# Packing the gains into the first transfer, holding the third feature tile's transfer, the first norm in the fifth chunk, and smaller store pieces in a two-layer trunk

## The chip, the cores and the metric

The kernel runs on one core of a Trainium2 chip. The metric is the device time of one execution in microseconds. The engines are called by these names: TensorE (PE, with its weight loads PEld), VectorE (DVE), ScalarE (ACT), GpSimd (POOL) and SyncE (SP). SP does no arithmetic here; it issues the loads and most of the stores, one behind the other, each as soon as what it waits for is there.

## The reference

There are 256 tokens of width 2048, and 16 learned tokens are put ahead of them, so L = 272. Layer 0 is differential attention with 8 heads, a partial rotary embedding and a SiLU gate; layer 1 is causal pooling over windows of 2, 4, 8 and 16 with a SiLU gate. Everything is 32-bit floating point.

```python
for i in range(DEPTH):                       # DEPTH = 2
    hn = rms_norm(h, pre_norm_g[i])
    if i % N_MIXERS == 0:
        y = diff_attention_mixer(hn, attn_w_in[j], attn_w_out[j], ...)
    else:
        y = pool_mixer(hn, pool_w_in[j], pool_w_group[j], pool_scale[j], pool_w_out[j])
    h = h + rms_norm(y, post_norm_g[i])
return h[:, N_META:]
```

`rms_norm(x, g)` is x / sqrt(mean(x²) + eps) · g. In the attention, `lam = exp(sum(lq1*lk1)) - exp(sum(lq2*lk2)) + lam_init` weighs the second softmax against the first.

## The kernel before

**Layout.** Features lie on the 128 partitions: the residual stream is 16 feature tiles (KT = 16) of 128 x 272. A weight chunk is 128 output features of one projection, 128 partitions x 2048 columns, 1 MB; the list `chunks` (lines 57 to 71) holds all of them in the order of their use: per head two chunks of q, two of k and two of v, then 16 of the gate, 16 of the output projection, then those of layer 1.

**Precision.** A 32-bit product is made of three matmuls on a faster type. Each operand is split into a head, rounded by ScalarE (`act.copy`, line 97), and a remainder, which VectorE gets by subtraction (line 98). `mm3` (lines 119 to 123) multiplies head by head, head by remainder and remainder by head.

**Chunks.** `load(i)` (line 75) issues the transfer of chunk i into one of two raw buffers, `split(i)` (line 84) makes head and remainder, three buffers each. A raw buffer comes free when VectorE has made the remainder; only then can the load of the chunk after the next one start. `rest[i]` is the instruction that makes the remainder.

**The front.** The first four chunks (q0, q1, k0, k1: `FIRST`) can't be multiplied before the feature tiles are there, so they come mixed with them: the tensor `first` holds for each feature tile 272 columns of activations and 4 x 128 columns of weights. Lines 203 to 206 load it in eleven transfers: activations and first weight block of tile 0, the rest of tile 0, tiles 1, 2 and 3 singly, then six pairs of tiles. The constants, 70 columns of gains and lambda vectors (`small`), come by a transfer on ScalarE's queue into `sp` (line 140). Six small matmuls on a tile of ones (`busy(6)`, line 193; each is two instructions) run while the first transfer is under way; the ones are written by GpSimd (line 147).

For each feature tile k (lines 226 to 245) ScalarE casts the weights (230) and the activations times their gain (234), VectorE makes both remainders (231, 235), and TensorE issues twelve matmuls (239 to 241) into four accumulators. The squares of the activations for the first norm are made on ScalarE (`square0`, line 224) and added up by VectorE (`fold`, line 107; the last sum is line 255).

**The first norm.** The projections are linear in the token's norm factor, so the norm is applied behind them: to the rotary tables and the gates. Chunks 4 and 5 (`NF`, `NF + 1`: the two v chunks of head 0) run with `run_part(i, a, n)`, which issues the 3 n matmuls of feature tiles a to a + n - 1. `Norm` (lines 157 to 186) takes the mean by matmuls against a column of ones (171), scales it on VectorE (174), raises it to -0.5 on GpSimd (181), and spreads the result over the partitions by matmuls (185). Line 262 copies it out of PSUM as `r0`, and lines 264 and 265 multiply the rotary tables by it; nothing of head 0 can be evacuated before that. The order around it:

```python
run_part(NF, 0, KT)
run_part(NF + 1, 0, 5)
norm0 = Norm(sq0, "pre0", rcol0)
with tc.issue_after(norm0.vi.ins):
    split(NF + 2)
run_part(NF + 1, 5, 7)
dve.tensor_copy(r0, norm0.spread())
```

**Order.** The builder lists the instructions of each engine in an order of its own, by the text's order and by what is ready. `with tc.issue_after(ins)` puts the instructions of the block that run on the same engine as `ins` behind it there. On the chip each engine then works its list off in order.

**The main loop.** From slot 6 on (lines 504 to 529) each slot is one chunk: its 48 matmuls (`proj`), then the evacuation of its result and a step of an earlier head. Slots 0 to 5 have their results already in `acc0`; for them only the evacuation runs.

**The end.** Layer 1's output projection gives two blocks of 128 tokens. For the second block (b = 1, lines 776 to 796) columns 0 to 511 go through TensorE and ScalarE and are stored by ScalarE; VectorE makes the other 1536 columns in three pieces of 640, 512 and 384 (lines 793 to 795), and SP stores each.

Of the kernel before, what the change touches and what calls it, by code (L numbers as in the profile page):

```python
# [40 lines left out]


@with_exitstack
def trunk(ctx: ExitStack, tc: tile.TileContext, first, hT, xt, small, gpost1, rope, w_in, w_out, p_in, p_grp, p_out, out):
    nc = tc.nc
    dve, act, pool, pe = nc.vector, nc.scalar, nc.gpsimd, nc.tensor

# [36 lines left out]
    def split(i, parts=1, dst=None):  # L84

        if i >= NCH or i in halves:
            return
        load(i, parts)
        if dst is None:
            hi = wpool.tile([P, CW], F32R, tag="hi", name=f"hi{i}")  # L90
            lw = wpool.tile([P, CW], F32R, tag="lo", name=f"lo{i}")
        else:
            hi, lw = dst
        w = CW // parts
        for q in range(parts):
            s = slice(q * w, (q + 1) * w)
            act.copy(hi[:, s], raw[i][:, s])  # L97
            rest[i] = dve.tensor_tensor(out=lw[:, s], in0=raw[i][:, s], in1=hi.bitcast(F32)[:, s], op=ALU.subtract)  # L98
        halves[i] = (hi, lw)
# [32 lines left out]
    def busy(n):  # L132

        ps = bank("busy")
        for _ in range(n):
            pe.matmul(ps[:, 0:P], ones, ones, start=True, stop=True)


    sp = const.tile([P, C_END], F32, name="sp")
    act.dma_start(sp, small)  # L140
    rp = const.tile([P, 2, L], F32, name="rp")
    ident = const.tile([P, P], F32, name="ident")
    pool.memset(ident, 0.0)
    pool.affine_select(out=ident, in_=ident, pattern=[[-1, P]], compare_op=ALU.not_equal, fill=1.0,
                       base=0, channel_multiplier=1)
    ones = const.tile([P, P], F32, name="ones")
    pool.memset(ones, 1.0)
    warm = const.tile([P, 1], F32, name="warm")
    act.square(warm, ones[:, 0:1])
    ones_r = const.tile([P, P], F32R, name="ones_r")  # L150
    pool.tensor_copy(ones_r, ones)
    mhalf = const.tile([P, 3], F32, name="mhalf")
# [4 lines left out]
    class Norm:  # L157
# [10 lines left out]
        def mean(self, sq):  # L168
            c = 505 if self.v is None else 508
            for j in range(3):  # L170
                self.last = pe.matmul(self.pb[:, c + j:c + j + 1], sq[:, WIN[j]:WIN[j] + P], ones[:, 0:1], start=True, stop=True)
            v = const.tile([P, 3], F32, tag="nv", name=f"v_{self.name}_{c}", bufs=2)
            if self.v is None:
                self.vi = dve.tensor_scalar(out=v, in0=self.pb[:, c:c + 3], scalar1=1.0 / D, scalar2=EPS, op0=ALU.mult, op1=ALU.add)
            else:
                dve.scalar_tensor_tensor(out=v, in0=self.pb[:, c:c + 3], scalar=1.0 / D, in1=self.v, op0=ALU.mult, op1=ALU.add)
            self.v = v
# [12 lines left out]
    xs = base.tile([P, 2, KT, L], F32R, tag="xs", name="xs")  # L190
    xh, xl = xs[:, 0], xs[:, 1]

    busy(6)
    x0 = ExitStack()
    xp = x0.enter_context(tc.tile_pool(name="xp", bufs=1))
    sq0 = const.tile([P, L], F32, tag="sq", name="sq0")


    NF = len(FIRST)
    pk = xp.tile([P, KT, L + NF * P], F32, name="pk")  # L200
    fhi = base.tile([P, KT, NF, P], F32R, tag="os", name="fhi")
    flo = (base.tile([P, KT // 2, NF, P], F32R, tag="big", name="flo0"), xp.tile([P, KT // 2, NF, P], F32R, name="flo1"))
    nc.sync.dma_start(pk[:, 0, 0:L + P], first[:, 0, 0:L + P])
    nc.sync.dma_start(pk[:, 0, L + P:], first[:, 0, L + P:])
    for a, b in ((1, 2), (2, 3), (3, 4), (4, 6), (6, 8), (8, 10), (10, 12), (12, 14), (14, 16)):
        nc.sync.dma_start(pk[:, a:b, :], first[:, a:b, :])
    load(NF)
    nc.sync.dma_start(rp, rope)
    load(NF + 1)
# [16 lines left out]
    for k in range(KT):  # L226
        hi, lw = fhi[:, k], flo[k // 8][:, k % 8]
        for i, n in ((0, 1), (1, NF - 1)) if k == 0 else ((0, NF),):
            w = pk[:, k, L + i * P:L + (i + n) * P].rearrange("p (i c) -> p i c", c=P)
            act.copy(hi[:, i:i + n], w)  # L230
            dve.tensor_tensor(out=lw[:, i:i + n], in0=w, in1=hi.bitcast(F32)[:, i:i + n], op=ALU.subtract)
            if i == 0:
                g = sp[:, C_PRE0 + k:C_PRE0 + k + 1]
                act.activation(xh[:, k, :], pk[:, k, 0:L], AF.Copy, scale=g)
                dve.scalar_tensor_tensor(out=xl[:, k, :], in0=pk[:, k, 0:L], scalar=g, in1=xh.bitcast(F32)[:, k, :],
                                         op0=ALU.mult, op1=ALU.subtract)
        for i in range(NF):
            o = acc0[i][:, 0:L]
            pe.matmul(o, hi[:, i], xh[:, k, :], start=k == 0, stop=False)  # L239
            pe.matmul(o, lw[:, i], xh[:, k, :], start=False, stop=False)  # L240
            pe.matmul(o, hi[:, i], xl[:, k, :], start=False, stop=k == KT - 1)
        if k >= 8:
            square0(k - 8)
        if k >= KT - 2:
            split_part(NF, slice((k - KT + 2) * (CW // 2), (k - KT + 3) * (CW // 2)))
# [2 lines left out]
    fold(s8[:, 0:8], s8[:, 0])  # L248
    for k in range(8, KT):
        square0(k)  # L250
    split(NF + 1)
    load(NF + 3)
    with tc.issue_after(rest[NF + 1].ins):
        fold(s8[:, 8:KT], s8[:, 8])
        dve.tensor_tensor(out=sq0, in0=s8[:, 0], in1=s8[:, 8], op=ALU.add)
    run_part(NF, 0, KT)
    run_part(NF + 1, 0, 5)
    norm0 = Norm(sq0, "pre0", rcol0)
    with tc.issue_after(norm0.vi.ins):
        split(NF + 2)  # L260
    run_part(NF + 1, 5, 7)
    dve.tensor_copy(r0, norm0.spread())

    dve.tensor_tensor(out=rp[:, 0, :], in0=rp[:, 0, :], in1=r0, op=ALU.mult)
    dve.tensor_tensor(out=rp[0:ROPE, 1, :], in0=rp[0:ROPE, 1, :], in1=r0[0:ROPE, :], op=ALU.mult)
    run_part(NF + 1, 12, 4)
    x0.close()
    l0 = ExitStack()
    att = l0.enter_context(tc.tile_pool(name="att", bufs=1))
# [2 lines left out]
    on = base.tile([P, KT, L], F32, tag="big", name="on")  # L272
    ssb = att.tile([P, NH, L], F32, name="ssb")


    lp = const.tile([P, 2], F32, name="lp")
    dve.tensor_tensor(out=lp, in0=sp[:, C_LAM:C_LAM + 2], in1=sp[:, C_LAM + 2:C_LAM + 4], op=ALU.mult)
    psl = bank("psl")
    pe.matmul(psl[:, 0:2], ones, lp, start=True, stop=True)
    le = const.tile([P, 2], F32, name="le")  # L280
    act.activation(le, psl[:, 0:2], AF.Exp)
    dve.scalar_tensor_tensor(out=lamc, in0=le[:, 0:1], scalar=LAM_INIT, in1=le[:, 1:2], op0=ALU.add, op1=ALU.subtract)

    sub = const.tile([P, 2], F32, name="sub")
    dve.tensor_scalar(out=sub, in0=sp[:, C_SUB:C_SUB + 2], scalar1=1.0 - LAM_INIT, scalar2=None, op0=ALU.mult)
# [218 lines left out]
    for slot in range(NH * 6 + KT):  # L504
        if slot < NH * 6:
            h, i = divmod(slot, 6)
            hd = heads[h]
            if i == 0:
                hd.h = h
                hd.qk = att.tile([P, 4, L], F32, name=f"qk{h}", tag="qk")  # L510
                hd.qs = att.tile([P, 2, 4, L], F32R, name=f"qs{h}", tag="qs")
                hd.qkh, hd.qkl = hd.qs[:, 0], hd.qs[:, 1]
                hd.qm = att.tile([P, 2, 2, 32], F32R, name=f"qm{h}", tag="qm")
                hd.sw = att.tile([ROPE, 4, L], F32, name=f"sw{h}", tag="sw")
                hd.vT = att.tile([P, 2, L], F32, name=f"vT{h}", tag="vT")
        if slot < 6:
            ps = acc0[slot]
        else:
            ps = bank(f"p{slot}")
            proj(ps, 0, L, xh, xl)  # L520

        if slot == NF + 2:
            with tc.issue_after(heads[0].done.ins):
                split(cur[0] + 1)
        elif slot != NF + 3:
            split(cur[0] + 1)
        load(cur[0] + 2)
        with tc.issue_after(rest[cur[0]].ins):
            after_proj(slot, ps)
# [246 lines left out]
    def out_store(b, y_last):  # L776
        i = 3 + b
        r = rf[:, b:b + 1]
        act.activation(r, part_s[:, b, i:i + 1], AF.Sqrt, scale=1.0 / D, bias=rm[:, b:b + 1])
        y_last()  # L780
        dve.reciprocal(r, r)
        if b:

            c = slice(0, 512)
            po = [bank(f"po{q}")[:, 0:256] for q in range(2)]
            for q in range(2):
                pe.matmul(po[q], ident, ht[:, b, 256 * q:256 * q + 256], start=True, stop=False)
            act.activation(diag, ident, AF.Copy, scale=r)
            for q in range(2):
                pe.matmul(po[q], diag, y[:, b, 256 * q:256 * q + 256], start=False, stop=True)  # L790
                act.copy(ht[:, b, 256 * q:256 * q + 256], po[q])
            act.dma_start(out[b * P:(b + 1) * P, c], ht[:, b, c])
        for c in (slice(512, 1152), slice(1152, 1664), slice(1664, D)) if b else (slice(0, 512), slice(512, 1280), slice(1280, D)):
            dve.scalar_tensor_tensor(out=ht[:, b, c], in0=y[:, b, c], scalar=r, in1=ht[:, b, c],
                                     op0=ALU.mult, op1=ALU.add)
            nc.sync.dma_start(out[b * P:(b + 1) * P, c], ht[:, b, c])
# [41 lines left out]
def _cols(v):  # L838
    return np.ascontiguousarray(np.asarray(v).reshape(-1, P).T)
# [49 lines left out]
```

## Time and profile before

| | us |
|---|---|
| median of 3 runs | 838.74 |
| lowest and highest run | 838.42, 839.45 |
| the profiled execution | 839.03 |
| its span, first to last instruction | 837.2 |
| TensorE busy in the span | 828.8 |
| VectorE, ScalarE, GpSimd busy | 584.9, 433.9, 6.2 |
| data moved | 149.35 MB, mean 178 GB/s |

The mean granted TensorE clock of the profiled execution is 0.999 of full speed. A row of the timeline reads: start in us from the span's start, duration in us, engine, line, operation, output and inputs with their shapes, count; in brackets the idle time of the engine ahead of it and what ended it. A row of the stretches of time reads: from and to, length, busy time (and instructions) of PE, PEld, DVE, ACT and POOL, granted clock, mean busy share of the 16 DMA engines, GB/s. A row of the waits reads: who waited for whom, us in total, times, longest.

### The profile page before, as it was taken

What the parts mean: (1) busy time and instruction counts of PE and PEld (TensorE: products, weight loads), DVE (VectorE), ACT (ScalarE), POOL (GpSimd) and SP (SyncE); (2) the same over time, 40 slices, a digit from 0 to 9 for tenths busy, and PEclk for the clock granted to TensorE, in tenths of its full rate; (3) what the DMA queues carried; (4) which work ended last, traced back from release to release, by engine and by line L of the source; (5) the groups of instructions that cost most, each with busy time, mean ns of one, the idle gap of its engine ahead of it and who ended that gap; (6) DMA issues with size and microseconds to landing.
All of it is one profiled execution on the core that took longest, in us unless ns stands there. A gap on an engine that the chain in (4) does not pass through costs nothing.

```text
span 837.2 us, 14470 instructions
## 1 busy us (share of the span) xinstructions
PE 828.8 (99%) x6072; PEld 798.2 (95%) x6072; DVE 584.9 (70%) x953; ACT 433.9 (52%) x674; POOL 6.2 (1%) x14
## 2 busy tenths in 40 slices
PE   8999999999999999999999999999999999999997
PEld 8999999999999999999999999999999888888886
DVE  6789777676858687897854644797998766775423
ACT  7646655554545465855445543554544445564422
POOL 0100000000000000000000000000000000000000
PEclk9999999999999999999999999999999999999999
DMA  9445444444444444355459754146556555545512
GB/s 350 175 151 200 153 151 155 154 158 164 159 165 156 152 151 151 117 186 189 164 178 379 272 184 151 51 158 245 176 194 263 180 195 201 182 169 201 202 51 100
DMA packets 22385, 149.35 MB, mean 178 GB/s; under 512 B 2608, under 2 KB 2992, under 8 KB 5552
## 3 DMA queue, kind: packets, MB, share of 16 engines
q1 hardware_dynamic: 22032, 148.14, 49.2%
q8 instruction: 47, 0.77, 0.4%
q10 hardware_dynamic: 288, 0.30, 0.1%
q14 instruction: 18, 0.15, 0.1%
HBM read 146.33 MB, written 2.10 MB: 177 GB/s over the span
## 4 chain that ended last, share of the span: by engine, by line
PE 98%; DMA 1%; POOL 0%; DVE 0%; ACT 0%; issue 0%; SPq 0%; DVEq 0%; ACTq 0%; POOLq 0%
PE p L121 14%; PE p L122 14%; PE p L123 14%; PE pv L129 7%; PE py L121 4%; PE py L123 4%; PE py L122 4%; PE pu L122 4%; PE pu L121 4%; PE pu L123 4%; PE pv L130 4%; PE pz L759 3%; PE pz L758 3%; PE pz L760 3%; PE pm L129 2%; PE pq L239 1%
## 5 line engine op out<-in xcount | busy, mean ns | idle before, releaser
L98 DVE TENSOR_TENSOR lo<-raw,hi 128x2048 fp32r<-128x2048 f32 (+1 forms) x123 | 279.1, 2270 | 137.4 <-ACT hi L97 137.2
L97 ACT CAST hi<-raw 128x2048 fp32r<-128x2048 f32 (+1 forms) x123 | 233.0, 1896 | 193.0 <-PE p L122 95.3
L121 PE MATMUL p<-xs,hi 128*128 128x272 f32 x928 | 270.2, 291 | 0.0
L123 PE MATMUL p<-xs,lo 128*128 128x272 f32 x928 | 268.3, 289 | 0.0
L122 PE MATMUL p<-xs,hi 128*128 128x272 f32 x928 | 267.5, 288 | 0.0
L122 PEld LDWEIGHTS p<-xs,hi 128*128 128x128 f32 x928 | 174.8, 188 | 0.0
L121 PEld LDWEIGHTS p<-xs,hi 128*128 128x128 f32 x928 | 174.8, 188 | 0.0
L123 PEld LDWEIGHTS p<-xs,lo 128*128 128x128 f32 x928 | 174.6, 188 | 0.0
L129 PE MATMUL pv<-hs,hi 128*128 128x512 f32 x256 | 89.5, 393 | 0.0
L121 PE MATMUL py<-os,hi 128*128 128x272 f32 x256 | 74.3, 290 | 0.0
L123 PE MATMUL py<-os,lo 128*128 128x272 f32 x256 | 74.1, 289 | 0.0
L122 PE MATMUL py<-os,hi 128*128 128x272 f32 x256 | 73.7, 288 | 0.0
L130 PE MATMUL pv<-hs,lo 128*128 128x256 f32 x256 | 71.8, 280 | 0.0
L123 PE MATMUL pu<-hs,lo 128*128 128x260 f32 (+3 forms) x224 | 63.7, 285 | 0.0
L122 PE MATMUL pu<-hs,hi 128*128 128x260 f32 (+3 forms) x224 | 63.6, 284 | 0.0
L121 PE MATMUL pu<-hs,hi 128*128 128x260 f32 (+3 forms) x224 | 63.6, 285 | 0.0
L129 PEld LDWEIGHTS pv<-hs,hi 128*128 128x128 f32 x256 | 48.0, 188 | 10.9
L122 PEld LDWEIGHTS py<-os,hi 128*128 128x128 f32 x256 | 48.3, 189 | 0.0
L121 PEld LDWEIGHTS py<-os,hi 128*128 128x128 f32 x256 | 48.2, 188 | 0.0
L123 PEld LDWEIGHTS py<-os,lo 128*128 128x128 f32 x256 | 48.2, 188 | 0.0
L130 PEld LDWEIGHTS pv<-hs,lo 128*128 128x128 f32 x256 | 48.1, 188 | 0.0
L760 PE MATMUL pz<-hi,zs 128*128 128x512 f32 (+1 forms) x120 | 45.0, 375 | 0.0
(248 smaller groups left out, 1319.0 us busy)
## 6 DMA issues: line engine op xcount, KB each, us to landing
raw<-in_w_in SPq DMA_DIRECT2D x60, 1024.0 KB, 4.8
raw<-in_p_in SPq DMA_DIRECT2D x29, 1024.0 KB, 4.8
raw<-in_w_out SPq DMA_DIRECT2D x16, 1024.0 KB, 4.9
raw<-in_p_out SPq DMA_DIRECT2D x14, 1024.0 KB, 4.8
pk<-in_first SPq DMA_DIRECT2D x6, 784.0 KB, 11.4
raw<-in_p_grp SPq DMA_DIRECT2D x4, 1024.0 KB, 4.8
rawu<-in_p_in SPq DMA_DIRECT2D x3, 1024.0 KB, 6.5
h<-in_hT SPq DMA_DIRECT2D x4, 544.0 KB, 7.2
```

Of the source, the lines that this page charges most:

```text
L97: act.copy(hi[:, s], raw[i][:, s])
L98: rest[i] = dve.tensor_tensor(out=lw[:, s], in0=raw[i][:, s], in1=hi.bitcast(F32)[:, s], op=ALU.subtract)
L121: pe.matmul(o, wh, xh, start=first, stop=False)
L122: pe.matmul(o, wh, xl, start=False, stop=False)
L123: pe.matmul(o, wl, xh, start=False, stop=last)
L129: pe.matmul(ps[:, 0:2 * n], wh, x, start=first, stop=False, skip_group_check=not first)
L130: pe.matmul(ps[:, 0:n], wl, x[:, 0], start=False, stop=last)
L239: pe.matmul(o, hi[:, i], xh[:, k, :], start=k == 0, stop=False)
L758: pe.matmul(ps, zh[:, k, s], wh[:, c], start=k == 0, stop=False)
L759: pe.matmul(ps, zh[:, k, s], wl[:, c], start=False, stop=False)
L760: pe.matmul(ps, zl[:, k, s], wh[:, c], start=False, stop=k == KT - 1)
```

## The change

- The 70 columns of constants are packed in front of tile 0 in the tensor `first`; the transfer on ScalarE's queue is gone. The gains of the front are read from the packed tile, and GpSimd copies all 70 columns to `sp` for the later users.
- Ahead of the transfer of the third feature tile GpSimd copies one element of the first piece to where that transfer will write. So the transfer, and what follows on SP, waits until the first piece has landed.
- The ones are written by VectorE instead of GpSimd, the warm-up has seven matmuls instead of six, and ScalarE's first activation stands behind the transfers in the text.
- The last sums of the squares come ahead of chunk 5's remainder on VectorE; the mean of the first norm is taken after eight feature tiles of chunk 4, and its spread after five more. Chunk 6's remainder follows the copy of `r0`. The matmul, exponential and sum that give lambda move into that stretch.
- Chunk 7's load and head are issued in slot 0 and its remainder in slot 4.
- The second block's store pieces are 256, 512, 512 and 256 columns.

```diff
     sp = const.tile([P, C_END], F32, name="sp")
-    act.dma_start(sp, small)
     rp = const.tile([P, 2, L], F32, name="rp")
+    ones = const.tile([P, P], F32, name="ones")
+    dve.memset(ones, 1.0)
...
-    ones = const.tile([P, P], F32, name="ones")
-    pool.memset(ones, 1.0)
     warm = const.tile([P, 1], F32, name="warm")
-    act.square(warm, ones[:, 0:1])
...
-    busy(6)
+    busy(7)
...
-    pk = xp.tile([P, KT, L + NF * P], F32, name="pk")
+    pks = xp.tile([P, C_END + KT * (L + NF * P)], F32, name="pk")
+    pk = pks[:, C_END:].rearrange("p (k c) -> p k c", k=KT)
...
-    nc.sync.dma_start(pk[:, 0, 0:L + P], first[:, 0, 0:L + P])
-    nc.sync.dma_start(pk[:, 0, L + P:], first[:, 0, L + P:])
-    for a, b in ((1, 2), (2, 3), (3, 4), (4, 6), (6, 8), (8, 10), (10, 12), (12, 14), (14, 16)):
-        nc.sync.dma_start(pk[:, a:b, :], first[:, a:b, :])
+    ends = [0, C_END + L + P] + [C_END + k * (L + NF * P) for k in (1, 2, 3, 4, 6, 8, 10, 12, 14, 16)]
+    for a, b in zip(ends, ends[1:]):
+        if a == ends[3]:
+
+            pool.tensor_copy(pks[:, a:a + 1], pks[:, 0:1])
+        nc.sync.dma_start(pks[:, a:b], first[:, a:b])
+    act.square(warm, ones[:, 0:1])
+    pool.tensor_copy(sp, pks[:, 0:C_END])
...
-    split(NF + 1)
+    fold(s8[:, 8:KT], s8[:, 8])
+    t = dve.tensor_tensor(out=sq0, in0=s8[:, 0], in1=s8[:, 8], op=ALU.add)
+    with tc.issue_after(t.ins):
+        split(NF + 1)
     load(NF + 3)
-    with tc.issue_after(rest[NF + 1].ins):
-        fold(s8[:, 8:KT], s8[:, 8])
-        dve.tensor_tensor(out=sq0, in0=s8[:, 0], in1=s8[:, 8], op=ALU.add)
-    run_part(NF, 0, KT)
-    run_part(NF + 1, 0, 5)
+    run_part(NF, 0, 8)
     norm0 = Norm(sq0, "pre0", rcol0)
-    with tc.issue_after(norm0.vi.ins):
-        split(NF + 2)
-    run_part(NF + 1, 5, 7)
-    dve.tensor_copy(r0, norm0.spread())
+    run_part(NF, 8, 5)
+    r0c = dve.tensor_copy(r0, norm0.spread())
...
-    run_part(NF + 1, 12, 4)
+    lp = const.tile([P, 2], F32, name="lp")
+    dve.tensor_tensor(out=lp, in0=sp[:, C_LAM:C_LAM + 2], in1=sp[:, C_LAM + 2:C_LAM + 4], op=ALU.mult)
+    run_part(NF, 13, 3)
+    with tc.issue_after(r0c.ins):
+        split(NF + 2)
+    psl = bank("psl")
+    pe.matmul(psl[:, 0:2], ones, lp, start=True, stop=True)
+    le = const.tile([P, 2], F32, name="le")
+    act.activation(le, psl[:, 0:2], AF.Exp)
+    dve.scalar_tensor_tensor(out=lamc, in0=le[:, 0:1], scalar=LAM_INIT, in1=le[:, 1:2], op0=ALU.add, op1=ALU.subtract)
+    run_part(NF + 1, 0, KT)
...
-        if slot == NF + 2:
+        if slot == 0:
+
+            i7 = cur[0] + 1
+            load(i7)
+            halves[i7] = (wpool.tile([P, CW], F32R, tag="hi", name=f"hi{i7}"), wpool.tile([P, CW], F32R, tag="lo", name=f"lo{i7}"))
+            act.copy(halves[i7][0], raw[i7])
+        elif slot == NF:
+            rest[i7] = dve.tensor_tensor(out=halves[i7][1], in0=raw[i7], in1=halves[i7][0].bitcast(F32), op=ALU.subtract)
+        elif slot == NF + 2:
...
-        for c in (slice(512, 1152), slice(1152, 1664), slice(1664, D)) if b else (slice(0, 512), slice(512, 1280), slice(1280, D)):
+        for c in (slice(512, 768), slice(768, 1280), slice(1280, 1792), slice(1792, D)) if b else (slice(0, 512), slice(512, 1280), slice(1280, D)):
```

More of the change, by code (lines that the diff above doesn't have):

```diff
@@ L43, in trunk @@
 @with_exitstack
-def trunk(ctx: ExitStack, tc: tile.TileContext, first, hT, xt, small, gpost1, rope, w_in, w_out, p_in, p_grp, p_out, out):
+def trunk(ctx: ExitStack, tc: tile.TileContext, first, hT, xt, gpost1, rope, w_in, w_out, p_in, p_grp, p_out, out):
     nc = tc.nc
@@ L173, in mean @@
             if self.v is None:
-                self.vi = dve.tensor_scalar(out=v, in0=self.pb[:, c:c + 3], scalar1=1.0 / D, scalar2=EPS, op0=ALU.mult, op1=ALU.add)
+                dve.tensor_scalar(out=v, in0=self.pb[:, c:c + 3], scalar1=1.0 / D, scalar2=EPS, op0=ALU.mult, op1=ALU.add)
             else:
@@ L232, in trunk @@
             if i == 0:
-                g = sp[:, C_PRE0 + k:C_PRE0 + k + 1]
+                g = pks[:, C_PRE0 + k:C_PRE0 + k + 1]
                 act.activation(xh[:, k, :], pk[:, k, 0:L], AF.Copy, scale=g)
@@ L273, in trunk @@
     ssb = att.tile([P, NH, L], F32, name="ssb")
[L276 to L282, printed above, removed]
     sub = const.tile([P, 2], F32, name="sub")
@@ L862 @@
     w_in = _tiles(A(attn_w_in)[0])
+    small = np.concatenate([
+        _cols(A(pre_norm_g)[0]), _cols(A(pre_norm_g)[1]), _cols(A(post_norm_g)[0]), _cols(A(pool_scale)[0]),
+        _cols(A(attn_subln_g)[0]), _cols(A(attn_lambda_q1)[0]), _cols(A(attn_lambda_q2)[0]),
+        _cols(A(attn_lambda_k1)[0]), _cols(A(attn_lambda_k2)[0])], axis=1)
     arrays = {
-        "first": np.ascontiguousarray(np.concatenate(
-            [hT] + [w_in[c].reshape(P, KT, P) for c in FIRST], axis=2)),
+        "first": np.ascontiguousarray(np.concatenate([small, np.concatenate(
+            [hT] + [w_in[c].reshape(P, KT, P) for c in FIRST], axis=2).reshape(P, -1)], axis=1)),
         "hT": hT,
         "xt": np.ascontiguousarray(A(x)[0]),
-        "small": np.ascontiguousarray(np.concatenate([
-            _cols(A(pre_norm_g)[0]), _cols(A(pre_norm_g)[1]), _cols(A(post_norm_g)[0]), _cols(A(pool_scale)[0]),
-            _cols(A(attn_subln_g)[0]), _cols(A(attn_lambda_q1)[0]), _cols(A(attn_lambda_q2)[0]),
-            _cols(A(attn_lambda_k1)[0]), _cols(A(attn_lambda_k2)[0])], axis=1)),
         "gpost1": np.ascontiguousarray(A(post_norm_g)[1:2]),
```

## The prediction, made before the changed kernel ran

> **What bounds the kernel now.** I read, in this order, the page, TensorE's waits, the timeline of the first 46 us engine by engine, the landing times of the first transfers, and the last 8 us.
>
> ```profile
> span 837.2 us, 14470 instructions
> PE 828.8 (99%) x6072; PEld 798.2 (95%) x6072; DVE 584.9 (70%) x953; ACT 433.9 (52%) x674; POOL 6.2 (1%) x14
> ```
> ```profile
> PE pq L239 <- ACT xs L234: 1.3, 2, 1.1
> PE busy L136 <- POOL ones L147: 1.1, 1, 1.1
> PE po L790 <- ACT diag L788: 0.7, 1, 0.7
> PE rms_pre L185 <- POOL rcol L181: 0.4, 1, 0.4
> ```
>
> TensorE is busy for 828.8 of 837.2 us. The change removes no matmul of the model, so it can only act on what TensorE does not do: four waits of 3.5 us together, and the end behind the last matmul. Everything below is therefore a sum of single microseconds on 839, and 0.2% is 1.7 us, about what a measurement of this kernel can tell from no change.
>
> The largest wait is 1.1 us, between the first and the second feature tile:
>
> ```profile
> 3.48 0.30 ACT L230 CAST fhi<-pk 128x128 fp32r<-128x128 f32 x1 [0.81 <-DMA pk<-in_first]
> 6.69 0.29 PE L241 MATMUL pq<-xs,fhi 128*128 128x272 f32 x1
> 6.98 0.62 ACT L230 CAST fhi<-pk 128x512 fp32r<-128x512 f32 x1 [1.77 <-DMA pk<-in_first]
> 8.07 0.65 PE L239 MATMUL pq<-xs,fhi 128*128 128x272 f32 x3 [1.09 <-ACT xs L234]
> ```
>
> The second tile lands at 6.96; ScalarE and the matmuls follow it by 1.1 us (6.98 to 8.07). From there TensorE never stops again until the first norm.
>
> **Part 1, the hold.** The transfer of the third tile waits until GpSimd has copied one element of the first piece; on SP all later loads queue behind it: seven more pieces, chunk 4, the rotary table, chunk 5. Rows for the copy, for issue and landing of the second tile, the third and the pair 4/5, and for the rate:
>
> ```profile
> 1.36 0.29 POOL L151 CAST ones_r<-ones 128x128 fp32r<-128x128 f32 x1
> ...
> L206 SPq DMA_DIRECT2D pk<-in_first x1: 424/424/424, 1.6 to 1.6; - x1
> DMA to landing us min/median/max: 5.3/5.3/5.3
> ...
> L206 SPq DMA_DIRECT2D pk<-in_first x1: 432/432/432, 2.1 to 2.1; - x1
> DMA to landing us min/median/max: 6.0/6.0/6.0
> ...
> L206 SPq DMA_DIRECT2D pk<-in_first x1: 432/432/432, 3.0 to 3.0; - x1
> DMA to landing us min/median/max: 8.0/8.0/8.0
> ```
> ```profile
> 2.00:3.30 1.30, 1.30 (x8) 1.30 (x8) 0.00 (x0) 0.66 (x2) 0.00 (x0) 1.00 0.92 291
> 3.30:5.00 1.70, 1.51 (x7) 1.21 (x7) 1.20 (x5) 1.35 (x4) 0.00 (x0) 1.00 0.90 213
> 5.00:7.00 2.00, 1.98 (x11) 1.76 (x9) 0.21 (x1) 0.23 (x2) 0.00 (x0) 1.00 0.96 350
> 7.00:20.00 13.00, 11.93 (x95) 11.93 (x96) 10.72 (x19) 12.48 (x29) 0.00 (x0) 1.00 1.03 424
> ```
>
> (The last number is GB/s.) From 2.0 to 7.0 some 1.44 MB move (378 + 362 + 700 KB), but only the first two tiles, 0.8 MB, have landed: about 0.65 MB of later pieces moved meanwhile. Without them the second tile needs 0.82 MB in all; 378 KB are there at 3.3, the rest at 213 GB/s takes 2.1 us: 5.4, landed at some 5.6. That is early enough (5.6 + 1.1 = 6.7, while the first tile's matmuls end at 6.98), so the wait of 1.09 goes.
>
> Late next is the third tile. The first piece is in when ScalarE starts at 3.48; the copy of one element is bounded by nothing and the 0.29 of GpSimd's cast of a 128x128 tile, and SP then issues at about 3.8 instead of 2.1. Its bytes flow from about 5.0. If it comes home with the same 0.65 MB of later pieces beside it, as the second tile does today, 1.05 MB at 350 to 424 GB/s put it at 7.5 to 8.0; today it lands at 8.1. TensorE could take it at 8.49 (6.98 + 12 matmuls of 0.126) and needs it landed by 7.4. Pair 4/5 stays near its 11.0, where TensorE today starts tile 4 at 12.6. So part of the 1.09 is kept: bounds -1.09 (the third tile lands within 3.6 us of its issue; the second piece took 2.9) and +0.6 (it needs the 5.3 that the second tile took: 9.1, matmuls at 10.2 instead of 9.58). I take **-0.5**, nearer to the rate rows.
>
> [...]
>
> **Part 2, packing the gains, the memset, the seventh warm-up matmul.** The 35 KB of gains leave ScalarE's queue and ride in front of the first piece, whose 200 KB become 235: at 291 GB/s up to 0.12 later, but the second transfer beside it is gone. The warm-up matmul needs `ones`, now written by VectorE (idle until 3.68) instead of GpSimd; 14 instructions instead of 12:
>
> ```profile
> 1.13 2.93 PE L136 MATMUL busy<-ones 128*128 128x128 f32 x12 [1.13 <-POOL ones L147]
> 3.68 0.16 DVE L277 TENSOR_TENSOR lp<-sp 128x2 f32<-128x2 f32 x1 [3.68 <-DMA sp<-in_small]
> ```
>
> At 0.24 each the two more take 0.49, from a start some 0.2 earlier, and end at 4.3, about where the first real matmul starts. Bounds -0.15 to +0.25; I take **+0.05**. The copy of the gains on GpSimd and the earlier lambda chain lie beside matmuls; nothing waits for them soon.
>
> **Part 3, the first norm.** Before, 15 matmuls of chunk 5, six for the mean, 21, then the six that spread the result:
>
> ```profile
> 30.76 0.28 PE L121 MATMUL pq<-xs,hi 128*128 128x272 f32 x1
> 38.70 0.72 PE L171 MATMUL rms_pre<-ones,sq 128*128 128x1 f32 x6
> 39.29 0.37 PE L121 MATMUL pq<-xs,hi 128*128 128x272 f32 x1
> 41.89 0.29 PE L123 MATMUL pq<-xs,lo 128*128 128x272 f32 x1
> 42.61 0.94 PE L185 MATMUL rms_pre<-ident,rcol 128*128 128x16 f32 x6 [0.44 <-POOL rcol L181]
> ...
> 39.77 2.78 POOL L181 TENSOR_TENSOR rcol<-v_pre,mhalf 128x3 f32<-128x3 f32 x1 [3.42 <-DVE v_pre L174]
> ...
> 531.56 0.85 POOL L181 TENSOR_TENSOR rcol<-v_post,mhalf 128x3 f32<-128x3 f32 x1 [489.00 <-DVE v_post L176]
> ```
> ```profile
> 27.31 2.36 DVE L216 TENSOR_TENSOR lo<-raw,hi 128x1024 fp32r<-128x1024 f32 x2
> 30.38 2.29 DVE L98 TENSOR_TENSOR lo<-raw,hi 128x2048 fp32r<-128x2048 f32 x1 [0.71 <-ACT hi L97]
> 32.59 2.52 DVE L107 TENSOR_TENSOR pk<-pk 128x1088 f32<-128x1088 f32 x3
> 35.14 0.44 DVE L255 TENSOR_TENSOR sq<-pk 128x272 f32<-128x272 f32 x1
> 39.46 0.16 DVE L174 TENSOR_SCALAR v_pre<-rms_pre 128x3 f32<-128x3 f32 x1 [3.88 <-PE rms_pre L171]
> ```
>
> 48 matmuls of chunk 4 and 15 of chunk 5 from 30.76 to 38.70 give 0.126 each. The cover today is 21 of them: they end at 42.02, the spread starts at 42.61, a gap of 0.59. The chain under it is VectorE's scaling (0.76 after the mean starts), then 3.15 to the spread, of which the power alone is 2.78. It is the first power of the run; the later one takes 0.85, and the first stays first. The change leaves 15 matmuls, 1.89, as cover in the text, against 2.65: that alone is 0.76 more idle time.
>
> Worse, VectorE: the remainder of chunk 5 (2.29) moves behind the fold, whose sum is then ready at 29.67 + 2.52 + 0.44 = 32.6. TensorE comes to the mean at 30.76 + 24 x 0.126 - 0.5 = 33.3. The remainder stands earlier in the text than the scaling and is ready, so VectorE runs it from 32.6 to 34.8 and the scaling waits: 34.8, power, spread at 37.95. TensorE has finished its 15 matmuls at 33.3 + 0.66 + 1.89 = 35.85: idle 2.1. Against that, the order written in the text isn't that of the engine:
>
> ```profile
> 4.77 0.43 ACT L224 ACTIVATE pk<-pk 128x272 f32<-128x272 f32 x1 [0.17 <-DVE xs L235]
> ```
>
> This square stands at tile 8 in the text and ran behind tile 0. The builder fills an engine with ready work, so some of the nine matmuls left of chunk 4 may stand ahead of the spread, up to 1.13 us. I take half: idle 1.55, so **+0.95** against 0.59; bounds -0.4 (scaling before the remainder, all nine ahead: 1.35 - 1.13) and +1.5.
>
> What follows has cover: chunk 6's first matmul moves from 2.4 to about 8 us behind the spread, while the evacuations gain time. Chunk 7's remainder, now behind the four evacuations, is due two chunks (12 us) on: 0, with 0.3 us at stake.
>
> **Part 4, the end.** The second block's pieces of 640, 512 and 384 columns become 256, 512, 512 and 256:
>
> ```profile
> L794 DVE SCALAR_TENSOR_TENSOR ht<-y,rf,ht 128x640 f32<-128x640 f32 x1 | 0.9, 884 | 0.0
> L794 DVE SCALAR_TENSOR_TENSOR ht<-y,rf,ht 128x384 f32<-128x384 f32 x1 | 0.6, 612 | 0.0
> ...
> 833.00:834.00 1.00, 0.00 (x0) 0.00 (x0) 0.00 (x0) 0.00 (x0) 0.00 (x0) 1.00 1.00 371
> 834.00:835.00 1.00, 0.00 (x0) 0.00 (x0) 0.00 (x0) 0.00 (x0) 0.00 (x0) 1.00 1.02 380
> ```
>
> The two give 0.136 per 128 columns, so 256 take 0.48 and the first store goes out 0.40 earlier; one more instruction makes the last 0.1 later. The DMA engines are full from 833 to 835, so the end follows the bytes (1 MB), and an earlier start counts: **-0.25**, bounds -0.4 and +0.1.
>
> **Sum.** -0.5 + 0.05 + 0.95 - 0.25 = +0.25 us. The profiled execution took 839.03 (span 837.2 and 1.8 around it); it lies 0.3 above the median of the runs, 838.74. 838.74 + 0.25 = 839.0.
>
> **The rivals.**
> (A) Faster: the builder covers the norm (-0.4), the hold keeps its 1.09, end -0.3: -1.8, **836.9**. For it: TensorE's order is the builder's; against it: the 2.78 of the power, and 0.59 idle with more cover today.
> (B) Slower: the held transfers are bound by their issue, not by bytes, and land later by the 1.7 that SP was held. Pair 4/5 lands at 12.7, tile 4 starts as far behind it as today (11.0 to 12.6), at 14.2, +1.6; with part 3 and the end, +2.3: **841.0**. It decides from a landing of pair 4/5 later than 11.5. Against it: 424 GB/s and full DMA engines from 7 on.
> (C) The hold doesn't do what it says: the second tile's packets are slow in themselves, it lands at 6.5 to 7 again, and the held pieces run behind it as before. Term 1 is 0, the sum +0.75: **839.5**. For it: 213 GB/s from 3.3 to 5.0 at a busy share of 0.90, so packets that take long; against it: the 0.65 MB moved ahead.
>
> [...]
>
> **Chances.** Forecast 0.46, A 0.24, C 0.18, B 0.12. Faster by over 0.2% (below 837.06) needs A at its centre or better and a little luck: 0.17. Slower by over 0.2% (above 840.4): B and the worst of C, 0.13. Between: 0.70. The range leaves out B and the better half of A's tail: 836.8 to 840.6; the forecast's own is 838.0 to 840.2.
>
> **What would show it.** Part 1: the second tile's cast before 6, no wait of 1.1 at L239; a new wait there at tile 2 or 4 is C or B. Part 3: the spread's wait for the power 1 to 2 us, and chunk 5's remainder ahead of the scaling on VectorE. Part 4: the last store's landing earlier by a quarter. I am wrong if the spread's wait is below 0.5 or the front's waits grow.

## The result and the profile after

| | before | after |
|---|---|---|
| median of the runs taken side by side | 839.45 | 845.77 |
| lowest and highest run | 838.42, 840.26 | 845.02, 846.36 |
| the profiled execution's span | 837.2 | 844.0 |

The changed kernel is slower: the ratio is 1.0079 (the two medians alone give 1.0075), with a 95% interval of 1.0068 to 1.0091. The time lies above the forecast, 839.0, and outside its range of 836.8 to 840.6.

The head of the page of the changed kernel:

```profile
span 844.0 us, 14483 instructions
...
PE 831.4 (99%) x6074; PEld 800.9 (95%) x6074; DVE 585.4 (69%) x955; ACT 433.7 (51%) x674; POOL 4.5 (1%) x15
```

TensorE's busy time grew by 2.6 us, for two more (warm-up) instructions; the span grew by 6.8. So one part is idle time and another is work that ran longer. TensorE's waits in the changed kernel:

```profile
PE pq L242 <- ACT xs L237: 5.9, 2, 5.2
PE busy L136 <- DVE ones L142: 1.0, 1, 1.0
PE po L801 <- ACT diag L799: 0.7, 1, 0.7
```

The wait for the first norm's power, 0.4 before, is gone. But the front's wait, 1.3 us before, is now 5.9, and 5.2 of it is one stop. The timeline of the changed kernel shows where (first real matmul, second tile, last matmuls ahead of the stop, third tile, and ScalarE ahead of that):

```profile
4.17 0.60 PE L242 MATMUL pq<-xs,fhi 128*128 128x272 f32 x1
7.57 0.65 PE L242 MATMUL pq<-xs,fhi 128*128 128x272 f32 x3 [0.75 <-ACT xs L237]
9.07 0.29 PE L244 MATMUL pq<-xs,fhi 128*128 128x272 f32 x1
14.54 0.59 PE L242 MATMUL pq<-xs,fhi 128*128 128x272 f32 x1 [5.19 <-ACT xs L237]
...
12.95 1.12 ACT L233 CAST fhi<-pk 128x512 fp32r<-128x512 f32 x2
```

TensorE finishes the second tile at 9.36 and starts the third at 14.54; ScalarE, busy nearly all the while with other tiles, casts the third one only at 12.95 or a little later. The issue row of the held transfer (start of the issue, then the time from there to the landing):

```profile
L207 SPq DMA_DIRECT2D pk<-in_first x1: 544/544/544, 3.6 to 3.6; - x1
DMA to landing us min/median/max: 8.8/8.8/8.8
```

It was issued at 3.6, only 1.5 us later than the 2.1 of before, but took 8.8 us instead of 6.0 and landed at 12.4. The reason stands in the builder's list for SP, whose head in the changed kernel is:

```
L207 DMA pk<-in_first 128x470        first piece
L207 DMA pk<-in_first 128x384        rest of tile 0
L207 DMA pk<-in_first 128x784 x2     tiles 1 and 3
L207 DMA pk<-in_first 128x1568 x2    pairs 4/5 and 6/7
L207 DMA pk<-in_first 128x784        tile 2, the held one
L207 DMA pk<-in_first 128x1568 x4    the other pairs
```

The builder saw a transfer that must wait for GpSimd and put the ready ones ahead of it; without the hold its list stands in the text's order. Tile 3 and two pairs, five times the bytes of the held tile, went out first, landing at 7.7, 9.6 and 11.4, and the DMA engines were moving 412 GB/s from 9 to 11 us while TensorE, which adds up the tiles of one accumulator in order, waited for the one tile behind them. The sentence above that "what follows on SP" waits too describes the text, not this list.

The stretches of the changed kernel show what came after (from, to, length, busy time and instructions of PE, PEld, DVE, ACT, POOL, granted clock, DMA share, GB/s):

```profile
9.00:11.00 2.00, 0.36 (x3) 0.13 (x2) 1.15 (x5) 1.58 (x5) 0.00 (x0) 1.00 1.00 412
11.00:13.00 2.00, 0.00 (x0) 0.00 (x0) 1.94 (x5) 2.00 (x6) 0.00 (x0) 0.99 1.01 419
13.00:15.00 2.00, 0.46 (x1) 0.29 (x1) 2.00 (x5) 2.00 (x6) 0.00 (x0) 0.50 1.04 433
15.00:17.00 2.00, 2.00 (x10) 1.99 (x10) 1.38 (x3) 2.00 (x6) 0.00 (x0) 0.50 1.00 414
17.00:19.00 2.00, 2.00 (x10) 2.00 (x10) 2.00 (x5) 2.00 (x6) 0.00 (x0) 0.50 1.05 434
19.00:21.00 2.00, 2.00 (x15) 2.00 (x14) 2.00 (x4) 2.00 (x6) 0.00 (x0) 0.80 0.97 402
```

From 13.0 to nearly 20 the granted clock is 0.50, and TensorE issues 10 matmuls in 2 us where other stretches hold 16 to 18. TensorE counts as busy there, which is why its busy time grew. In this trace TensorE is idle from 9.36 and the half clock begins at 13.0, 3.6 us later; the full clock is back at about 19.8, some 5.2 us after the restart at 14.54.

### The profile page after: what moved, and what is told of

It reads as the page before. It is cut to its first block, busy times and chain, and to the rows that moved or that the text cites. A ratio compares the mean times of both kernels' runs of the same rounds, so it can differ in the third digit from the quotient of the medians.

```text
span 844.0 us, 14483 instructions
## 1 busy us (share of the span) xinstructions
PE 831.4 (99%) x6074; PEld 800.9 (95%) x6074; DVE 585.4 (69%) x955; ACT 433.7 (51%) x674; POOL 4.5 (1%) x15
## 4 chain that ended last, share of the span: by engine, by line
PE 97%; ACT 1%; DMA 1%; DVE 0%; SPq 0%; issue 0%; DVEq 0%; ACTq 0%
PE p L121 14%; PE p L122 14%; PE p L123 14%; PE pv L129 7%; PE py L121 4%; PE py L123 4%; PE py L122 4%; PE pu L122 4%; PE pu L123 4%; PE pu L121 4%; PE pv L130 4%; PE pz L771 3%; PE pz L770 3%; PE pz L769 3%; PE pm L129 2%; PE pq L242 1%
```

## The experiments

The theory after this reading: the hold costs everything, by the place that the builder gives the held transfer in SP's list. The rivals: the wait for GpSimd itself; one of the other parts; or the slower clock as something of its own. Each experiment was timed beside the kernel before on the same chip; that kernel's median was 838.71 beside the kernels without the hold, with the hold in order, with the hold alone and with the warm matmuls, and 838.66 beside the other four.

### Without the hold

```diff
-        if a == ends[3]:
-
-            pool.tensor_copy(pks[:, a:a + 1], pks[:, 0:1])
         nc.sync.dma_start(pks[:, a:b], first[:, a:b])
```

> The change without the copy that holds the third tile; SP then issues the eleven pieces in the order of the text. My theory (the builder put tile 3 and the pairs 4/5 and 6/7 ahead of the held third tile, TensorE waits 5.2 us for it and then runs 6.8 us at half clock): both vanish, TensorE's waits in the front are about 1 us as before, and the time is 0.5 to 1.5 us below the kernel before, about 838 where that has 839. Rival (the norm or the packing costs the time, the wait for tile 2 only moved it): 2 us or more above the kernel before remain.

Measured: 837.77 (837.23 to 838.23), ratio 0.9983, interval 0.9975 to 0.9992. Everything but the hold together is worth some 0.9 us, and the hold costs 845.77 - 837.77 = 8.0. (These two kernels were not timed side by side; by their distances from the kernel before, 6.3 above it and 0.9 below it, the hold costs 7.3.) This kernel is faster than both. TensorE's waits in it, then its timeline from chunk 4 to the first norm:

```profile
PE pq L239 <- ACT xs L234: 1.5, 1, 1.5
PE busy L136 <- DVE ones L142: 1.0, 1, 1.0
PE po L798 <- ACT diag L796: 0.7, 1, 0.7
```
```profile
30.46 0.29 PE L121 MATMUL pq<-xs,hi 128*128 128x272 f32 x1
33.48 0.72 PE L169 MATMUL rms_pre<-ones,sq 128*128 128x1 f32 x6
36.04 0.83 PE L183 MATMUL rms_pre<-ident,rcol 128*128 128x16 f32 x6
...
32.08 2.29 DVE L98 TENSOR_TENSOR lo<-raw,hi 128x2048 fp32r<-128x2048 f32 x1
34.28 0.15 DVE L172 TENSOR_SCALAR v_pre<-rms_pre 128x3 f32<-128x3 f32 x1
...
34.52 0.87 POOL L179 TENSOR_TENSOR rcol<-v_pre,mhalf 128x3 f32<-128x3 f32 x1 [1.50 <-DVE v_pre L172]
```

The mean takes 0.66 from 33.48 and the 15 matmuls behind it 1.89: 36.03, and the spread starts at 36.04. There is no gap. The scaling did wait behind chunk 5's remainder (32.08 to 34.37) as the prediction had it, but the power took 0.87 instead of 2.78. Chunk 4 starts 0.30 earlier than before (30.46 against 30.76) and the norm's gap of 0.59 is gone: 0.9 together. The list of waits holds nothing else of the front or the first slots, so the new places of chunk 7's load and remainder cost TensorE nothing here; the packing was not timed by itself.

The traces of the two kernels place most of the hold's 8.0 us. The third tile's first matmul here, and the mean in the changed kernel:

```profile
9.36 0.29 PE L239 MATMUL pq<-xs,fhi 128*128 128x272 f32 x1
```
```profile
41.27 0.72 PE L169 MATMUL rms_pre<-ones,sq 128*128 128x1 f32 x6
```

The second tile's matmuls end at about 9.3 in both; the third tile starts at 14.54 in the changed kernel and at 9.36 in this one, 5.2 later; from there to the norm's mean the changed kernel needs 41.27 - 14.54 = 26.7 us, this one 33.48 - 9.36 = 24.1: 2.6 more, the price of the half clock.

### The hold, with the list in the text's order

Every transfer behind the held one is put behind it on SP.

```diff
+    held = None
...
-        nc.sync.dma_start(pks[:, a:b], first[:, a:b])
+        with (tc.issue_after(held.ins) if held else ExitStack()):
+            d = nc.sync.dma_start(pks[:, a:b], first[:, a:b])
+        if a >= ends[3]:
+            held = d
...
-    load(NF)
-    nc.sync.dma_start(rp, rope)
-    load(NF + 1)
+    with tc.issue_after(held.ins):
+        load(NF)
+        nc.sync.dma_start(rp, rope)
+        load(NF + 1)
```

> The change with the hold as its text reads: every later transfer is put behind the held one on SP. My theory: no wait of 5 us, no half clock; the third tile, issued at about 3.8, lands at 7.5 to 8, TensorE waits up to 1 us for it, time 0 to 1.5 us below the kernel before. [...] Rival (a held transfer is late by itself, wherever it stands in the queue): the third tile still lands after 10 and the time stays 4 us or more above.

Measured: 839.48 (839.02 to 839.88), ratio 1.0006, interval 0.9997 to 1.0015. The held transfer's row and that of pair 4/5, the cast of tile 3, which ScalarE has to wait for, and the stretches of this kernel:

```profile
L209 SPq DMA_DIRECT2D pk<-in_first x1: 327/327/327, 3.7 to 3.7; - x1
DMA to landing us min/median/max: 3.9/3.9/3.9
...
L209 SPq DMA_DIRECT2D pk<-in_first x1: 432/432/432, 4.5 to 4.5; - x1
DMA to landing us min/median/max: 7.6/7.6/7.6
```
```profile
10.26 0.62 ACT L238 CAST fhi<-pk 128x512 fp32r<-128x512 f32 x1 [1.19 <-DMA pk<-in_first]
```
```profile
9.00:11.00 2.00, 1.88 (x12) 1.65 (x12) 0.87 (x3) 0.81 (x3) 0.00 (x0) 1.00 0.96 383
11.00:13.00 2.00, 1.86 (x11) 1.31 (x11) 1.02 (x2) 1.57 (x5) 0.00 (x0) 1.00 1.03 430
13.00:15.00 2.00, 1.98 (x13) 1.56 (x13) 1.97 (x4) 2.00 (x5) 0.00 (x0) 1.00 1.00 417
15.00:17.00 2.00, 2.00 (x18) 2.00 (x17) 1.93 (x5) 2.00 (x6) 0.00 (x0) 1.00 1.04 433
```

This is the kernel that the prediction's first part described. The held tile lands at 3.7 + 3.9 = 7.6, inside the 7.5 to 8.0 foretold, and no stop of 5 us is left. Against the kernel without the hold it still loses 1.7 us: tile 3 lands at 10.2 instead of 8.6, pair 4/5 at 12.1 instead of 10.5, and TensorE gets through 11 to 13 matmuls per 2 us from 9 to 15 where it could do 18, in gaps so short that the busy time hardly shows them. So the hold gains nothing even in the order that was meant, and the order turns 1.7 into 8.0.

### The hold alone, in the kernel before

```diff
+        if a == 2:
+            pool.tensor_copy(pk[:, 2, 0:1], pk[:, 0, 0:1])
         nc.sync.dma_start(pk[:, a:b, :], first[:, a:b, :])
```

> The kernel before with the hold alone (one element of tile 0 copied to tile 2's place). My theory: here too the held transfer falls behind tile 3 and pairs on SP's list, TensorE waits 5 us or more for tile 2 and is throttled afterwards: 6 to 8 us above the kernel before. Rival (the loss comes from the hold together with the packing or the norm): less than 3 us above.

Measured: 847.77 (847.28 to 848.22), ratio 1.0105, interval 1.0091 to 1.0118. TensorE's wait for the front, and the held transfer's row:

```profile
PE pq L241 <- ACT xs L236: 7.2, 3, 5.3
```
```profile
L208 SPq DMA_DIRECT2D pk<-in_first x1: 328/328/328, 3.8 to 3.8; - x1
DMA to landing us min/median/max: 9.5/9.5/9.5
```

The builder puts tile 3 and two pairs ahead here too; the tile lands at 13.3 and TensorE stops for 5.3 us. The hold needs no other part of the change to do its damage: 9.1 us here.

### The list's order alone, without any wait

```diff
-    for a, b in zip(ends, ends[1:]):
+    cuts = list(zip(ends, ends[1:]))
+    cuts.insert(6, cuts.pop(3))
+    for a, b in cuts:
-        if a == ends[3]:
-
-            pool.tensor_copy(pks[:, a:a + 1], pks[:, 0:1])
         nc.sync.dma_start(pks[:, a:b], first[:, a:b])
```

> The packed kernel without the hold, but with the third tile's transfer written behind tile 3 and pairs 4/5 and 6/7, in the place that the builder gave it in the changed kernel. No transfer waits for GpSimd. Theory (the place in SP's list costs the time, not the wait): the third tile lands at 12 to 12.5, TensorE waits 4.5 to 5.3 for it, the clock falls to 0.5 behind the wait, 845 to 846. Rival (the wait for GpSimd delays SP and what is behind it): 837.8 to 839.5.

Measured: 845.58 (844.96 to 846.55), ratio 1.0082, interval 1.0068 to 1.0095: within 0.2 us of the changed kernel's time. The third tile's matmul in this kernel:

```profile
14.57 0.59 PE L241 MATMUL pq<-xs,fhi 128*128 128x272 f32 x1 [5.76 <-ACT xs L236]
```

No transfer waits for GpSimd here, and the third tile starts within 0.03 us of the changed kernel's. Taken with the experiment that kept the wait and restored the order, this settles it: the place in the list causes the stop of 5 us, not the wait. The wait by itself costs the 1.7 us above.

### Warm matmuls in the stop

Twenty warm-up matmuls (40 instructions) are put behind the second tile's last matmul in the changed kernel.

```diff
-            pe.matmul(o, hi[:, i], xl[:, k, :], start=False, stop=k == KT - 1)
+            t = pe.matmul(o, hi[:, i], xl[:, k, :], start=False, stop=k == KT - 1)
+        if k == 1:
+            with tc.issue_after(t.ins):
+                busy(20)
```

> The change with 20 more warm-up matmuls (40 instructions, some 4.5 us of work that feeds nothing) behind tile 1's matmuls. If the half clock of 13.0 to 19.8 us follows from the idle time: tile 2 still starts at about 14.5, the granted clock stays at 1.00, and the time is 2.0 to 2.6 us below the changed kernel (about 843.3 where that has 845.8). Rival (the throttle comes from elsewhere, or the matmuls behind are bound by their operands): no difference from the changed kernel.

Measured: 843.23 (843.09 to 843.73), ratio 1.0052, interval 1.0038 to 1.0065. The stretches of this kernel, and its third tile:

```profile
13.00:15.00 2.00, 0.73 (x6) 0.56 (x5) 2.00 (x5) 2.00 (x5) 0.00 (x0) 1.00 1.03 430
15.00:17.00 2.00, 2.00 (x18) 2.00 (x17) 1.37 (x4) 2.00 (x6) 0.00 (x0) 1.00 1.02 420
```
```profile
14.44 0.77 PE L242 MATMUL pq<-xs,fhi 128*128 128x272 f32 x4 [1.27 <-ACT xs L237]
```

The third tile starts as late as in the changed kernel, but the clock stays at 1.00 and 18 matmuls fit into 2 us. The time is 2.5 us below the changed kernel's 845.77, which was timed apart from it; that agrees with the 2.6 read from the two timelines: the half clock follows from the stop and is not a cause of its own.

### The power away from VectorE's sum, and beside it

Two experiments turn on the power's 2.78 us. In the kernel before, chunk 6's remainder runs on VectorE from 39.54 to 41.83, beside the power's 39.77 to 42.55:

```profile
39.54 2.29 DVE L98 TENSOR_TENSOR lo<-raw,hi 128x2048 fp32r<-128x2048 f32 x1
```

The first edit keeps that remainder away from the power's start:

```diff
     with tc.issue_after(norm0.vi.ins):
+        gap = dve.memset(pk[:, 0:2, L:L + 512], 0.0)
+    with tc.issue_after(gap.ins):
         split(NF + 2)
```

> The kernel before, with one VectorE memset (128x1024, into feature tiles that are no longer read) put between the first norm's scaling and chunk 6's remainder, so that the remainder no longer starts beside the first GpSimd power. It adds about 0.9 us to VectorE, which has nothing due there. Theory (the power is long in the kernel before because VectorE's two-input remainder runs beside it: 39.54 to 41.83 beside 39.77 to 42.55): the power takes 0.85 to 0.9, TensorE's wait of 0.4 for it is gone, the end comes 0.4 to 0.6 earlier, about 838.2 against 838.7. Rival (the first power of a run is long wherever it stands, as the prediction had it): 2.78 again, no change of the time.

The second puts a sum of two SBUF tiles beside the power in the kernel without the hold, where the power was short:

```diff
-                dve.tensor_scalar(out=v, in0=self.pb[:, c:c + 3], scalar1=1.0 / D, scalar2=EPS, op0=ALU.mult, op1=ALU.add)
+                self.vi = dve.tensor_scalar(out=v, in0=self.pb[:, c:c + 3], scalar1=1.0 / D, scalar2=EPS, op0=ALU.mult, op1=ALU.add)
...
     norm0 = Norm(sq0, "pre0", rcol0)
+    with tc.issue_after(norm0.vi.ins):
+        w = pk[:, 0:4, L:L + 512]
+        dve.tensor_tensor(out=w, in0=w, in1=pk[:, 4:8, L:L + 512], op=ALU.add)
```

> The packed kernel without the hold, with one VectorE sum of two tiles in SBUF (128x2048, on feature tiles that are no longer read) put right behind the first norm's scaling, so that it stands beside the power; that sum's result is not used. Theory (two-input VectorE work beside the power): the power takes 2.3 to 2.9 instead of 0.87, the spread finds 15 matmuls (1.9 us) between and TensorE waits 1.0 to 1.5; 838.8 to 839.3 against 837.8. Rival (a power has 2.78 in the kernel before for another reason): 0.87 again and 837.8.

The power in the first of these kernels:

```profile
41.20 0.86 POOL L181 TENSOR_TENSOR rcol<-v_pre,mhalf 128x3 f32<-128x3 f32 x1 [39.52 <-DVE v_pre L174]
```

and, in the second, the power, the sum, the spread, and a later stop:

```profile
34.62 2.76 POOL L179 TENSOR_TENSOR rcol<-v_pre,mhalf 128x3 f32<-128x3 f32 x1 [30.93 <-DVE v_pre L172]
...
34.38 2.28 DVE L260 TENSOR_TENSOR pk<-pk 128x2048 f32<-128x2048 f32 x1
...
37.43 0.93 PE L183 MATMUL rms_pre<-ident,rcol 128*128 128x16 f32 x6 [1.17 <-POOL rcol L179]
...
60.99 0.39 PE L121 MATMUL p<-xs,hi 128*128 128x272 f32 x1 [1.08 <-DVE e L389]
```

The first power of the run takes 0.86 with a memset beside it and 2.76 with a two-input sum beside it. In the second kernel it ends at 37.38, 0.72 after the sum's end at 36.66; in the kernel before it ends at 42.55, 0.72 after the remainder's end at 41.83. This fits a GpSimd that stands still until VectorE's instruction is through, so that its span hides a wait; that is a reading of the two ends, and why GpSimd would wait is not shown.

The times: 838.11 (837.40 to 840.17) for the first, ratio 0.9994, interval 0.9985 to 1.0003. The middle is the 0.5 us expected, but no change lies inside the interval; what is shown is the power, not the gain. The second: 840.80 (840.52 to 841.08), 3.0 above the kernel without the hold, two to three times what was expected. The spread's wait, 1.17, is as expected; the new stop of 1.08 at 61 us is not. TensorE waits there for VectorE's sum of the first head's scores, which VectorE runs at 60.64, behind a remainder that it started at 58.36; that it is late by the added sum and the late copy of `r0` is likely, but was not tried apart. By that matmul the whole difference has come about: it starts 2.82 later than its like in the kernel without the sum (58.17), and the spans differ by 2.8.

### The store pieces alone, in the kernel before

```diff
-        for c in (slice(512, 1152), slice(1152, 1664), slice(1664, D)) if b else (slice(0, 512), slice(512, 1280), slice(1280, D)):
+        for c in (slice(512, 768), slice(768, 1280), slice(1280, 1792), slice(1792, D)) if b else (slice(0, 512), slice(512, 1280), slice(1280, D)):
```

> The kernel before with the last rows' store pieces alone changed (256, 512, 512 and 256 columns). The prediction's fourth term: -0.25, so 838.45. Theory from the traces (the first store goes out 0.4 earlier, the last one 0.2 later, and 7.8 us lie from the last output product to the end in all kernels): 0.0, within 0.1 of the kernel before, 838.7.

Measured: 838.87 (838.31 to 839.73), ratio 1.0003, interval 0.9994 to 1.0012. The interval still takes in the quarter microsecond foretold, so the traces, one execution of each kernel, have to decide: the span and the last output product in this kernel, then that product in the kernel before, whose span is 837.2.

```profile
span 836.8 us, 14473 instructions
...
828.91 0.28 PE L760 MATMUL pz<-hi,zs 128*128 128x256 f32 x1
```
```profile
829.41 0.28 PE L760 MATMUL pz<-hi,zs 128*128 128x256 f32 x1
```

From the start of that product to the end are 836.8 - 828.9 = 7.9 us here and 837.2 - 829.4 = 7.8 in the kernel before; in the changed kernel, where it starts at 836.2, they are 7.8 as well. No gain is to be seen.

## Why the prediction was wrong

**Part 1, the hold (-0.5): the step that failed.** It says that "on SP all later loads queue behind it: seven more pieces, chunk 4, the rotary table, chunk 5". That was read from the text. The builder moved three transfers, with five times its bytes, ahead of the held one, and the term was +8.0, of which the traces show 5.2 of idle time and 2.6 at half clock. The prediction had the knowledge in hand: for the first norm it says that "the builder fills an engine with ready work" and shows a square of ScalarE that ran eight tiles early. It applied this to TensorE and left SP out.

The working that follows from that step was right on one point and wrong on the other. In the order assumed, the held tile lands at 7.6, as worked out. But the term would not have been -0.5 there; it is +1.7, and it comes by rival B's mechanism: pair 4/5 lands at 12.1, past the 11.5 from which B was to decide (foretold 12.7 and +1.6). The prediction held pair 4/5 to be "near its 11.0", by the full rate of the DMA engines. In the run tile 3 and pair 4/5 were issued 1.4 and 1.5 later than without the hold, and both landed 1.6 later: pair 4/5 took 7.6 us from its issue to its landing here and 7.5 without the hold. So its landing followed its issue. From 9 to 11 us the DMA engines moved 383 GB/s at a busy share of 0.96 here, against 417 at 1.00 without the hold; what set the rate was not traced.

Whether the second tile lands earlier when less is issued behind it stays open. Its landing lay at 6.9, 6.6, 6.8, 6.6, 6.0 and 5.9 in the profiled executions of the six kernels without a hold, and at 6.4, 5.8, 5.8 and 7.5 in the four with one. Only the kernel with the hold in the text's order had nothing behind the second tile, and its 5.8 is hardly less than the 5.9 of a kernel with all pieces behind. The 0.65 MB moved ahead, on which the -0.5 rests, is thus no proof of a delay; one execution of each is too little to settle it. The packed rows show no delay of pair 4/5: it lands at 10.5 in the packed kernel without the hold, and at 11.0 in the kernel before.

**Part 2 (+0.05): within its bounds.** The first real matmul starts at 4.17 instead of 4.26. The 0.30 by which chunk 4 begins earlier without the hold goes with the second tile's landing (6.6 against 6.9), which scatters by more than that.

**Part 3, the first norm (+0.95): wrong sign; measured -0.59.** In the kernel without the hold the chain was right up to the power: the remainder ahead, the scaling behind it at 34.3 (foretold 34.8). The size of one term was wrong. "It is the first power of the run ... and the first stays first" explained 2.78 us by its place in the run. The row quoted there and the remainder row of VectorE (39.54, 2.29) stand side by side in the trace of before; the cause was the neighbour, and the change takes the neighbour away. The fifteen matmuls of the text were cover enough.

**Part 4, the end (-0.25): measured 0.** Counted from the last output product, SP sends the first store 0.4 earlier, but the last one 0.2 later, behind one more instruction, and the 7.8 us stay. That the DMA engines were full (a busy share of 1.00 to 1.02 from 833 to 835 us before) did not make an earlier start count.

**Sum.** With the measured terms, without the hold: -0.30 - 0.59 + 0 = -0.9, which gives 837.8 from 838.71 (measured 837.77); the -0.30 is the difference of two single executions. With the hold's 5.2 + 2.6 = 7.8 on top, that is 845.6 (measured 845.77).

## What to carry to other kernels

Where a tool orders the instruction lists, an added wait can change the order of the queue that it stands in, the DMA queue too: read the built list, and pin the followers if the wait is meant to hold them. A long instruction is not always a slow one (the power took 2.78 beside a two-input remainder, 0.86 and 0.87 without one): before its length is carried over to a new place, look at what ran beside it on the other engines. And a stop of TensorE is to be priced with the clock behind it: here 2.6 us on top of a stop of 5.2.

## What the runs showed beside that

The clock can fall after a much shorter pause. In the profiled execution of the kernel with the memset, TensorE paused for 1.76 us ahead of the second tile, and the stretches of that execution show:

```profile
6.00:7.00 1.00, 0.23 (x2) 0.02 (x1) 0.00 (x0) 0.10 (x1) 0.00 (x0) 1.00 1.03 361
7.00:8.00 1.00, 0.01 (x1) 0.01 (x1) 0.45 (x1) 0.94 (x2) 0.00 (x0) 1.00 0.96 364
8.00:9.00 1.00, 1.00 (x6) 1.00 (x7) 0.99 (x3) 0.99 (x3) 0.00 (x0) 0.69 1.06 420
9.00:10.00 1.00, 1.00 (x6) 1.00 (x6) 0.85 (x3) 1.00 (x4) 0.00 (x0) 0.50 0.99 401
...
11.00:12.00 1.00, 1.00 (x7) 1.00 (x6) 0.02 (x1) 0.94 (x3) 0.00 (x0) 0.60 1.05 433
12.00:13.00 1.00, 1.00 (x10) 1.00 (x9) 0.97 (x2) 1.00 (x3) 0.00 (x0) 1.00 0.99 414
```

The clock halves at about 8.4 and is back by 12. That execution took 840.17, against a median of 838.11 for its kernel, and its ten other runs lie between 837.40 and 838.73. Pauses of 1.09 in the kernel before, 1.50 in the kernel without the hold and 1.27 in the kernel with the warm matmuls left the clock at 1.00. So the front's wait of one to two microseconds may cost nothing in one execution and some 2 us in another; what decides was not tried.

TensorE also runs at about half rate in the first microseconds (in the kernel before its matmuls start 0.23 us apart near 5 us and 0.13 apart from 6.4 on), where the profile's granted clock reads 1.00. In the kernel before, rows of one matmul last 0.43 us, as in the changed kernel's half-clock stretch, up to about 6.2, and 0.29 from 6.4 on; in the kernel without the hold, rows of 0.29 stand from 4.45 on. The first tile's matmuls end at 6.98 there and at 6.25 here. So the second tile, which lands 0.3 earlier in the kernel without the hold, is waited for longer, 1.50 against 1.09: the wait that the hold was to remove depends on the start of one execution, too.
